# An encoder layer in split float32: weight slots of 1024 columns, 64-byte pads, and scale vectors and x loaded in quarters from another queue

## The chip, the core and the metric

The kernel runs on one core of a Trainium2 chip. The metric is the device time of one execution in microseconds (us), less is better. Three runs of the kernel before took 1114.95, 1115.65 and 1116.01 us, so the median is 1115.65 us. In the profile, PE is TensorE (matmuls), PEld its weight loads, DVE VectorE, ACT ScalarE, POOL GpSimd and SP the queue that issues most DMAs.

## The reference: what is computed

One layer on 256 rows of 2048 numbers, all float32:

```python
xn   = rmsnorm(x, pre_mix_gain)
proj = xn @ w_in                              # 2048 -> 3*1024 (hyena) + 832 (MLA)
y_hyena = x0 * long_conv(x1 * v, filters)     # by products with DFT tables
y_attn  = mla(c_q, c_kv, k_pe)                # 8 heads
mixed = concat(rmsnorm(y_hyena), rmsnorm(y_attn)) @ w_out        # 2048 x 2048
h  = x + rmsnorm(mixed, post_mix_gain)
gu = rmsnorm(h, pre_ffn_gain) @ w_up                             # 2048 x 11264
f  = (gelu(dwconv(gu[:, :5632])) * gu[:, 5632:]) @ w_down        # 5632 x 2048
y  = h + rmsnorm(f, post_ffn_gain)
```

## The kernel before, in words

Every operand of a large product is split into a high part (`...h`, or index 0) and a rest (`...l`, or index 1), and a product is three matmuls: high by high, high by rest, rest by high. In a matmul one operand is stationary (a 128x128 tile, loaded into the array by a PEld instruction ahead of each matmul) and the other is moving (it streams through, 256 or 512 columns here).

Weights come in tiles of 128 x 1024 float32 (512 KB). `stage` loads one with a DMA on SP into a slot `raw`, ACT copies it into a slot `wh` (L140), DVE subtracts to fill a slot `wl` (L143). There are four slots of each kind, used in turn; a slot is filled again when its last reader is done. The slots `wh` and `wl` are `W_SLOT` = 1040 columns wide, 4160 bytes in each partition, of which 1024 columns are used.

The stages, in order of time, with PE's work in them:

- MLA projection (to 52 us): `mm3` (L100 to L102), x stationary, weights moving.
- Hyena projection `hi` (52 to 262 us): `wm3` (L113 to L115), weights `why` stationary, x (`xT`) moving, 256 columns each; 48 weight tiles of 24 matmuls. Attention and the DFT products of the long convolution run between them.
- `w_out` (259 to 357 us), in two halves of 1024 output columns: `mm3`, the normalised mixer output (`mix`) stationary, weights moving, 512 columns; 12 matmuls for each of 16 tiles in a half.
- Residual and norm (352 to 381 us): `row_finish`, `post_mix`; they read the scale vectors `gbm` and `gbn` and the residual x (in tiles `h`).
- `w_up` (358 to 860 us): for n from 1 on, `wmm` (L108: 512 columns; L109: 256 columns), weights `wup` stationary, `hnT` moving; four weight tiles for each of 43 n, 64 matmuls.
- `w_down` (860 to 1105 us): `mm3` as in `w_out`, `fT` stationary, weights moving, 512 columns; 2 halves of 44 tiles, 12 matmuls each.

Each engine runs its instructions in the order in which the code emits them; the chains of attention and hyena are generators that are advanced between weight tiles (`turn`). POOL has, in this order around 250 to 300 us: sums of squares `sqh` (L547), the DMA of `gbm` (L873), `sqh`, the DMA of `gbn` (L875), `sqh`, two powers (L154) for the norm of the hyena output, and two DMAs of x into `h` (L877). A DMA whose target was used by earlier tiles waits for their readers, and what is behind it on its queue waits too.

Of the kernel before, what the change touches and what calls it, by code (L numbers as in the profile page):

```python
# [12 lines left out]
F32 = mybir.dt.float32  # L13
F32R = mybir.dt.float32r
# [4 lines left out]
P = 128  # L19
D = 2048  # L20
S = 256
# [7 lines left out]
NF = DFF // P  # L29
# [20 lines left out]
V_FCB = 274  # L50
V_ALL = 318
V_PAD = 320
W_SLOT = 1024 + 16


def _body(ctx, tc, a):
    nc = tc.nc
# [6 lines left out]

    const = ctx.enter_context(tc.tile_pool(name="const", bufs=1))
    edge = ctx.enter_context(tc.tile_pool(name="edge", bufs=1, side="right"))
    edge.tile([P, 24], F32, name="edge")
    wp = ctx.enter_context(tc.tile_pool(name="wp", bufs=4))
    psA = ctx.enter_context(tc.tile_pool(name="psA", bufs=2, space=bass.MemoryType.PSUM))
    psB = ctx.enter_context(tc.tile_pool(name="psB", bufs=3, space=bass.MemoryType.PSUM))  # L70
# [59 lines left out]

    def load(src, n, name):
        raw = wp.tile([P, 1024], F32, tag="raw", name=name)
        nc.sync.dma_start(raw[:, :n], src)
        return raw

    def split_w(raw, n, name, pool=None, cut=None):
        pool = pool or wp
        h = pool.tile([P, W_SLOT], F32R, tag="wh", name=name + "h")
        l = pool.tile([P, W_SLOT], F32R, tag="wl", name=name + "l")
        box["cast"] = nc.scalar.copy(h[:, :n], raw[:, :n])  # L140
        for e, o in ((nc.vector, slice(0, cut or n)), (nc.gpsimd, slice(cut or n, n))):
            if o.start < n:
                box["lo"] = e.tensor_tensor(l[:, o], raw[:, o], h[:, o].bitcast(F32), op=ALU.subtract)  # L143
        return h, l
# [21 lines left out]
    box = {}  # L166
# [13 lines left out]
    yp = l_stack.enter_context(tc.tile_pool(name="yp", bufs=1, side="left"))  # L180
    spec = l_stack.enter_context(tc.tile_pool(name="spec", bufs=1, side="left"))
    xTp = l_stack.enter_context(tc.tile_pool(name="xTp", bufs=1, side="left"))
    xT = [xTp.tile([P, 2, 2, P], F32R, name=f"xT{k}") for k in range(KD)]
    ya = [yp.tile([P, S], F32, name=f"ya{i}") for i in range(8)]
    yh = [yp.tile([P, S], F32, name=f"yh{i}") for i in range(8)]
# [15 lines left out]
    x = a["x"]  # L201
# [114 lines left out]
    for k in range(KD):  # L316
# [7 lines left out]
        wh, wl = wm[k]  # L324
# [423 lines left out]
    def channel_norm(sq, ys, gv, mix, nm, ps):  # L748

        rb = ps(f"rb{nm}")  # L750
        ps = ps(f"css{nm}")
        for b in range(2):
            nc.tensor.matmul(ps[:, b : b + 1], lhsT=sq[:, b * P : (b + 1) * P], rhs=ones[:, 0:1],
                             start=True, stop=True)
        r = [rms_scale(ps[:, b : b + 1], 1024, f"rn{nm}{b}", mixp) for b in range(2)]
        yield
        if nm == 'a':
            yield from pause(4)
        for b in range(2):
            bcast_rows(rb, r[b], b, mixp, "n" + nm)  # L760
        for i in range(8):
            with tc.issue_after(box["lo"].ins):
                nc.vector.scalar_tensor_tensor(ys[i], ys[i], vc(gv + i), rb[:, 0:S], op0=ALU.mult, op1=ALU.mult)
                split((mix[i][:, 0, :], mix[i][:, 1, :]), ys[i])
            if nm == "a" and i in (1, 3, 5):
                yield
# [3 lines left out]
    def attention_chain():  # L770
        nonlocal mixp, mix
        yield from latents()
        yield from attention()
        yield from pause(2)
        at_stack.close()
        mixp = mix_stack.enter_context(tc.tile_pool(name="mixp", bufs=1, side="right"))
        mix = [mixp.tile([P, 2, S], F32R, name=f"mix{k}") for k in range(KD)]
        yield from channel_norm(sqa, ya, V_AG, mix[0:8], "a", mi)

    mixp = mix = None  # L780
# [6 lines left out]
    for i, gi in order:  # L787
        for c in range(2):
            ps = (acc if cv else mj)(f"hi{i}{gi}{c}")[:, :S]
            for kh in range(2):  # L790
                wh, wl = stage(a["w_hy"][i, gi, c, kh], 1024, f"why{i}{gi}{c}{kh}")
                for kk in range(8):
                    k = kh * 8 + kk
# [8 lines left out]
    def row_units(wname, nk, half, lT, ps, hold, held):  # L802
        def get(k):
            return stage(a[wname][half, k], 1024, f"{wname}{half}{k}")

        nxt = get(0)
        for k in range(nk):
            w, nxt = nxt, get(k + 1) if k + 1 < nk else None
            for b in range(2):
                if b == 1 and k >= nk - hold:  # L810
                    held.append((k, w))
                    continue
                for c in range(2):
                    row_emit(ps[b][c], lT, k, b, w, c, nk)
            yield
# [38 lines left out]
    units = row_units("w_out", KD, 0, mix, psw, 0, None)  # L854
# [8 lines left out]
    h = [hp.tile([P, D], F32, name=f"h{b}") for b in range(2)]  # L863
    rb2 = hp.tile([P, S], F32, name="rb2")
    hn_stack = es()
    hnp = hn_stack.enter_context(tc.tile_pool(name="hnp", bufs=1, side="left"))
    hnTq = [hnp.tile([P, 4, 2, 2, P], F32R, name=f"hnT{c}") for c in range(4)]
    hnT = [hnTq[k // 4][:, k % 4] for k in range(KD)]
    pm_stack = es()
    pm = pm_stack.enter_context(tc.tile_pool(name="pm", bufs=1, side="left"))  # L870
    up0 = pm_stack.enter_context(tc.tile_pool(name="up0", bufs=4, side="left"))
    gbm = pm.tile([P, D], F32, name="gbm")
    nc.gpsimd.dma_start(gbm, a["post_mix_gain"].partition_broadcast(P))  # L873
    gbn = pm.tile([P, D], F32, name="gbn")
    nc.gpsimd.dma_start(gbn, a["pre_ffn_gain"].partition_broadcast(P))  # L875
    for b in range(2):
        nc.gpsimd.dma_start(h[b], x[b * P : (b + 1) * P, :])  # L877
    tmp = [pm.tile([P, D], F32, name=f"tmp{b}") for b in range(2)]
    ssq = [small(pm, 4, name=f"ssq{b}") for b in range(2)]
    ss2 = [small(pm, 4, name=f"ss2{b}") for b in range(2)]  # L880
    for _ in units:
        pass
    for b in range(2):
        for c in range(2):
            row_finish(psw, 0, b, c, gbm, tmp, ssq, pm)
# [26 lines left out]
    held = []  # L912
    psw = row_banks(1, "wo1")
    for k, _ in enumerate(row_units("w_out", KD, 1, mix, psw, HOLD, held)):
        if k == KD - HOLD - 2:
            first = [stage(a["w_up"][0, kq], 1024, f"wup0{kq}", up0) for kq in range(4)]
    row_finish(psw, 1, 0, 0, gbm, tmp, ssq, pm)
# [12 lines left out]
    fq = fpa_stack.enter_context(tc.tile_pool(name="fq", bufs=2, side="right"))  # L930
    fpa = fpa_stack.enter_context(tc.tile_pool(name="fpa", bufs=1, side="right"))
    NFA = 12
    def gated_tiles(pool, ks):
        for k in ks:
            if k % 4 == 0:
                pool.tile([P, 16], F32, name=f"fpad{k}")
            yield pool.tile([P, 2, S], F32R, name=f"fT{k}")

    fT = list(gated_tiles(fpa, range(NFA)))

    def up_tail(n, pg, pu):

# [49 lines left out]
    for n in range(1, NF):  # L992
        if n == 4:
            fpb = fpa_stack.enter_context(tc.tile_pool(name="fpb", bufs=1, side="right"))
            fT += gated_tiles(fpb, range(NFA, NF))
        new = (mi, mj) if n % 2 else (acc, acc)
        pg, pu = as4(new[0](f"pg{n}")), as4(new[1](f"pu{n}"))
        chs = []
        for kq in range(4):
            with es() as hold:  # L1000
                if n == 1:
                    for eng in range(2):
                        hold.enter_context(tc.issue_after(box[int(kq >= 2), 3, eng].ins))
                chs.append(stage(a["w_up"][n, kq], 1024, f"wup{n}{kq}"))
        for which, ps in ((0, pg), (1, pu)):
            for k in range(KD):
                wh, wl = chs[k // 4]
                o = (k % 4) * 256 + which * P
                wmm(ps, wh[:, o : o + P], wl[:, o : o + P], hnT[k], k == 0, k == KD - 1)
        up_tail(n, pg, pu)  # L1010
# [136 lines left out]
```

## Time and profile before

| | |
|---|---|
| median of three runs | 1115.65 us |
| the profiled execution | 1114.86 us, of which the span is 1113.1 us |
| PE busy | 1096.4 us (99%), 6334 matmuls |
| PEld busy | 959.4 us (86%) |
| DVE, ACT, POOL busy | 725.8 us (65%), 574.3 us (52%), 122.3 us (11%) |
| granted TensorE clock, mean | 0.997 |
| DMA | 207 MB, 186 GB/s over the span |

A share of the span is a mean over stages with different limits. A matmul's recorded time runs from its start to the end of its pipeline and overlaps the next one; what it costs in a row of matmuls is the distance from its start to the next start. The recorded times of two matmuls of one shape differ by as much as these distances do.

### The profile page before, as it was taken

To read this page: it belongs to the slowest core of one execution; us is meant where nothing else is said; L and a number is where in the kernel's file an instruction comes from. 1 tells how busy PE (TensorE), PEld (TensorE's weight loads), DVE (VectorE), ACT (ScalarE), POOL (GpSimd) and SP (SyncE) were. 2 spreads that over 40 slices of the span, in tenths; PEclk is the share of its full clock that TensorE was granted. 3 is DMA by queue.
4 is the path that set the end of the run, shared out by engine and by line. 5 is a ranking of instruction groups with operands and counts; after the bars stand their busy time and mean duration, and the time that the engine had idled before them with its cause. 6 is when DMAs were issued, how large, how long until landed. Compare 5 with 4: busy or idle time off the path is not lost.

```text
span 1113.1 us, 16496 instructions
## 1 busy us (share of the span) xinstructions
PE 1096.4 (99%) x6334; PEld 959.4 (86%) x6334; DVE 725.8 (65%) x1051; ACT 574.3 (52%) x884; POOL 122.3 (11%) x154
## 2 busy tenths in 40 slices
PE   9999999999999999999999999999999999999997
PEld 7899999998787888888888888888888888888885
DVE  7898878889567766666666666565756444454444
ACT  7756656655454646454545455554545333343332
POOL 4300100011002311111111111111111000000000
PEclk9999999999999999999999999999999999999999
DMA  9664445444775354645464645555555766666652
GB/s 312 224 212 148 161 133 171 143 136 131 276 253 189 114 190 162 216 157 219 156 214 164 204 176 197 182 188 191 179 199 172 258 188 191 189 192 188 189 191 95
DMA packets 59207, 207.23 MB, mean 186 GB/s; under 512 B 6903, under 2 KB 7801, under 8 KB 58489
## 3 DMA queue, kind: packets, MB, share of 16 engines
q1 hardware_dynamic: 57832, 200.39, 54.1%
q0 software_dynamic: 720, 5.24, 1.3%
q8 instruction: 49, 0.80, 0.3%
q10 hardware_dynamic: 576, 0.56, 0.1%
q14 instruction: 30, 0.24, 0.1%
HBM read 204.07 MB, written 2.10 MB: 185 GB/s over the span
## 4 chain that ended last, share of the span: by engine, by line
PE 86%; issue 6%; DVE 5%; DMA 1%; POOL 1%; ACT 1%; DVEq 0%; POOLq 0%; SPq 0%; ACTq 0%
PE pg L108 14%; PE pu L108 14%; PE pg L109 7%; PE pu L109 7%; PE wd L102 7%; PE wd L100 7%; PE wd L101 7%; PE hi L113 4%; PE hi L115 4%; PE hi L114 4%; DMA w_out<-in_w_out 1%; POOL tmp L893 1%; PE y L499 1%; PE pq L101 1%; PE pq L100 1%
## 5 line engine op out<-in xcount | busy, mean ns | idle before, releaser
L91 ACT CAST fT<-u 128x256 fp32r<-128x256 f32 x44 | 17.8, 406 | 111.1 <-DVE u L952 111.0
L551 DVE SCALAR_TENSOR_TENSOR t<-g,vec,t 128x255 f32<-128x255 f32 x44 | 21.3, 483 | 63.8 <-ACT t L550 63.8
L948 POOL TENSOR_TENSOR u<-u,rb 128x256 f32<-128x256 f32 x44 | 32.4, 736 | 276.4 <-DVE u L125 276.4
L550 ACT ACTIVATE t<-g,vec 128x256 f32<-128x256 f32 x44 | 26.5, 603 | 54.9 <-POOL g L946 54.9
L125 DVE TENSOR_TENSOR g<-pg,jg 128x256 f32<-128x256 f32 x44 | 18.7, 424 | 52.5 <-ACT jg L124 52.5
L946 POOL TENSOR_TENSOR g<-g,rb 128x256 f32<-128x256 f32 x44 | 32.4, 736 | 137.6 <-DVE g L125 136.2
L124 ACT COPY jg<-pg 128x256 f32<-128x256 f32 x44 | 16.3, 371 | 54.7 <-PE pg L109 54.7
L952 DVE TENSOR_TENSOR u<-u,t 128x256 f32<-128x256 f32 x44 | 18.7, 424 | 36.4 <-POOL u L948 35.4
L834 POOL TENSOR_TENSOR rw0r<-rw0v,neghalf 128x1 f32<-128x1 f32 x2 | 1.1, 558 | 292.1 <-DVE rw0v L831 292.1
L92 DVE TENSOR_TENSOR fT<-u,fT 128x256 fp32r<-128x256 f32 x44 | 18.7, 425 | 19.8 <-ACT fT L91 19.8
L553 DVE SCALAR_TENSOR_TENSOR t<-g,vec,t 128x255 f32<-128x255 f32 x44 | 21.3, 484 | 1.5
L547 POOL TENSOR_TENSOR sqa<-sqa,sqa 128x256 f32<-128x256 f32 x7 | 6.8, 965 | 128.9 <-ACT sqa L546 128.6
L951 ACT ACTIVATE t<-t 128x256 f32<-128x256 f32 x44 | 18.2, 414 | 2.7 <-DVE t L553 2.7
L125 DVE TENSOR_TENSOR u<-pu,ju 128x256 f32<-128x256 f32 x44 | 18.3, 417 | 0.0
L550 ACT ACTIVATE cv<-z,vec 128x256 f32<-128x256 f32 x24 | 14.4, 601 | 7.5 <-DVE z L616 7.5
L232 POOL TENSOR_TENSOR sqx<-sqx,sqx 128x256 f32<-128x256 f32 x15 | 15.7, 1047 | 17.8 <-ACT sqx L231 17.6
L124 ACT COPY ju<-pu 128x256 f32<-128x256 f32 x44 | 16.0, 364 | 0.0
L96 DVE SCALAR_TENSOR_TENSOR xT<-xraw,vec,xT 128x256 fp32r<-128x256 f32 x16 | 11.8, 740 | 2.7 <-ACT xT L95 2.7
L893 POOL TENSOR_TENSOR tmp<-h,gbn 128x512 f32<-128x512 f32 x8 | 13.3, 1682 | 2.4 <-DVE h L890 2.4
L616 DVE TENSOR_TENSOR z<-hi,rbx 128x256 f32<-128x256 f32 x24 | 10.0, 418 | 5.2 <-PE hi L115 4.9
L547 POOL TENSOR_TENSOR sqh<-sqh,sqh 128x256 f32<-128x256 f32 x7 | 7.8, 1114 | 47.6 <-ACT sqh L546 47.5
L553 DVE SCALAR_TENSOR_TENSOR cv<-z,vec,cv 128x255 f32<-128x255 f32 x24 | 12.4, 518 | 0.2
(3679 smaller groups left out, 4378.0 us busy)
## 6 DMA issues: line engine op xcount, KB each, us to landing
wup<-in_w_up SPq DMA_DIRECT2D x176, 512.0 KB, 4.8
w_down<-in_w_down SPq DMA_DIRECT2D x88, 512.0 KB, 3.5
why<-in_w_hy SPq DMA_DIRECT2D x48, 512.0 KB, 3.9
w_out<-in_w_out SPq DMA_DIRECT2D x32, 512.0 KB, 4.3
wm<-in_w_mla SPq DMA_DIRECT2D x16, 416.0 KB, 4.9
win<-in_window SPq DMA_DIRECT2D x8, 256.0 KB, 3.1
wuq<-in_w_uqn SPq DMA_DIRECT2D x4, 512.0 KB, 3.5
wkv<-in_w_ukv SPq DMA_DIRECT2D x4, 512.0 KB, 4.1
```

What stands on the lines that cost most here:

```text
L100: ins = nc.tensor.matmul(ps, lhsT=lh, rhs=rh, start=first, stop=False)
L101: nc.tensor.matmul(ps, lhsT=lh, rhs=rl, start=False, stop=False)
L102: nc.tensor.matmul(ps, lhsT=ll, rhs=rh, start=False, stop=last)
L108: nc.tensor.matmul(ps, lhsT=wh, rhs=xt, start=first, stop=False)
L109: nc.tensor.matmul(ps[:, :, 0, :], lhsT=wl, rhs=xt[:, :, 0, :], start=False, stop=last)
L113: nc.tensor.matmul(ps, lhsT=wh, rhs=xt[:, :, 0, :], start=first, stop=False)
L114: nc.tensor.matmul(ps, lhsT=wh, rhs=xt[:, :, 1, :], start=False, stop=False)
L115: box["mm"] = nc.tensor.matmul(ps, lhsT=wl, rhs=xt[:, :, 0, :], start=False, stop=last)
L125: nc.vector.tensor_add(d, ps4[:, :, 0, :], lo)
L550: nc.scalar.activation(dst, src, AF.Identity, bias=vc(bv), scale=vc(wv + 1))
L553: nc.vector.scalar_tensor_tensor(dst[:, : S - 1], src[:, 1:], vc(wv + 2), dst[:, : S - 1], op0=ALU.mult, op1=ALU.add)
L946: nc.gpsimd.tensor_tensor(g, g, rb2, op=ALU.mult)
```

## The change

`W_SLOT` goes: the slots `wh` and `wl` become 1024 columns, 4096 bytes. Pads of 16 columns (64 bytes) are allocated ahead of `xT` and `hnT`, behind `mix` and behind the first twelve `fT`; the pad at the right edge grows from 24 to 40 columns, and a pad ahead of every four `fT` goes. So the addresses of nearly all tiles move by multiples of 64 bytes. No arithmetic, no matmul and no copy is added or removed, and PE, DVE and ACT have the same instructions in the same order.

Counted from the addresses that the two built programs give, here is the byte address of the moving operand minus that of the stationary one, modulo 256, in matmuls of each stage:

| stage | before | after |
|---|---|---|
| MLA projection | 0, 64, 128, 192, a quarter each | 192 |
| `hi` (1152 matmuls) | 0 (312), 64 (288), 128 (264), 192 (288) | 64 |
| DFT products `K`, `AB`, `yc` (144) | 0 | 64 |
| `w_out` (384) | 0, 64, 128, 192, a quarter each | 0 |
| `w_up`, n from 1 on (2752) | 0, 64, 128, 192, a quarter each | 64 |
| `w_down` (1056) | 0, 64, 128, 192, a quarter each | 0 |

Before, the distance is the same within a weight tile and changes with the slot, by 64 from one tile to the next. In `w_up` the tiles of one n (`wup80`, `wup81`, `wup82`, `wup83` for n = 8) have the distances 128, 192, 0 and 64. In `w_out`, the tiles 0 and 1 of the second half (`w_out10` and `w_out11`; the first digit is the half) have 0 and 192. In `w_down`, the tiles 1 and 2 of the first half (`w_down01`, `w_down02`) have 64 and 0. In `hi`, `why2001` has 0, and `why2101` and `why1200` both have 64.

The second part: `gbm`, `gbn` (1 MB each) and x (2 MB into `h`) are loaded by SP in quarters of the vectors and halves of x's row blocks, one behind each of twelve `w_out` loads, and no longer by POOL in four whole DMAs.

```diff
-W_SLOT = 1024 + 16
...
-    edge.tile([P, 24], F32, name="edge")
+    edge.tile([P, 40], F32, name="edge")
...
-        nc.sync.dma_start(raw[:, :n], src)
+        box["load"] = nc.sync.dma_start(raw[:, :n], src)
...
-        h = pool.tile([P, W_SLOT], F32R, tag="wh", name=name + "h")
-        l = pool.tile([P, W_SLOT], F32R, tag="wl", name=name + "l")
+        h = pool.tile([P, 1024], F32R, tag="wh", name=name + "h")
+        l = pool.tile([P, 1024], F32R, tag="wl", name=name + "l")
...
+    xTp.tile([P, 16], F32, name="xpad")
     xT = [xTp.tile([P, 2, 2, P], F32R, name=f"xT{k}") for k in range(KD)]
...
         mix = [mixp.tile([P, 2, S], F32R, name=f"mix{k}") for k in range(KD)]
+        mixp.tile([P, 16], F32, name="mpad")
...
+    hnp.tile([P, 16], F32, name="hpad")
     hnTq = [hnp.tile([P, 4, 2, 2, P], F32R, name=f"hnT{c}") for c in range(4)]
...
-    nc.gpsimd.dma_start(gbm, a["post_mix_gain"].partition_broadcast(P))
     gbn = pm.tile([P, D], F32, name="gbn")
-    nc.gpsimd.dma_start(gbn, a["pre_ffn_gain"].partition_broadcast(P))
-    for b in range(2):
-        nc.gpsimd.dma_start(h[b], x[b * P : (b + 1) * P, :])
+
+    def piece(dst, src, c, n):
+
+        o = slice(c * n, (c + 1) * n)
+        with tc.issue_after(box["load"].ins):
+            nc.sync.dma_start(dst[:, o], src[:, o])
...
-    for _ in units:
-        pass
+    for k, _ in enumerate(units):
+        if k < 4:
+            piece(gbm, a["post_mix_gain"].partition_broadcast(P), k, 512)
...
     for k, _ in enumerate(row_units("w_out", KD, 1, mix, psw, HOLD, held)):
+        if k < 4:
+            piece(h[k // 2], x[k // 2 * P : (k // 2 + 1) * P, :], k % 2, 1024)
+        elif k < 8:
+            piece(gbn, a["pre_ffn_gain"].partition_broadcast(P), k - 4, 512)
...
-    def gated_tiles(pool, ks):
-        for k in ks:
-            if k % 4 == 0:
-                pool.tile([P, 16], F32, name=f"fpad{k}")
-            yield pool.tile([P, 2, S], F32R, name=f"fT{k}")
-
-    fT = list(gated_tiles(fpa, range(NFA)))
+    fT = [fpa.tile([P, 2, S], F32R, name=f"fT{k}") for k in range(NFA)]
+    fpa.tile([P, 16], F32, name="fpad")
```

POOL's order before, from the second half of the sums of squares to the scaling of the residual:

```order
L547 TENSOR_TENSOR sqh_124<-sqh_124,sqh5_3394 128x256
L873 DMA gbm_3854<-in_post_mix_gain 128x2048
L547 TENSOR_TENSOR sqh_124<-sqh_124,sqh6_3691 128x256
L875 DMA gbn_3856<-in_pre_ffn_gain 128x2048
L547 TENSOR_TENSOR sqh_124<-sqh_124,sqh7_3696 128x256
L154 TENSOR_TENSOR rnh0r_3759<-rnh0v_3757,neghalf_77 128x1
L154 TENSOR_TENSOR rnh1r_3763<-rnh1v_3761,neghalf_77 128x1
L877 DMA h0_3838<-in_x 128x2048
L877 DMA h1_3839<-in_x 128x2048
L834 TENSOR_TENSOR rw0r_4320<-rw0v_4318,neghalf_77 128x1
```

The same place of POOL in the changed kernel:

```order
L547 TENSOR_TENSOR sqh_125<-sqh_125,sqh5_3396 128x256
L547 TENSOR_TENSOR sqh_125<-sqh_125,sqh6_3693 128x256
L547 TENSOR_TENSOR sqh_125<-sqh_125,sqh7_3698 128x256
L153 TENSOR_TENSOR rnh0r_3761<-rnh0v_3759,neghalf_77 128x1
L153 TENSOR_TENSOR rnh1r_3765<-rnh1v_3763,neghalf_77 128x1
L835 TENSOR_TENSOR rw0r_4331<-rw0v_4329,neghalf_77 128x1
```

The four DMAs are gone from POOL, and the sums and powers stand behind one another.

SP's order before, at the loads of the first tiles of the second half of `w_out` (`w_out11` is tile 1 of half 1):

```order
L133 DMA w_out11_4028<-in_w_out 128x1024
L133 DMA w_out12_4046<-in_w_out 128x1024
L133 DMA w_out13_4064<-in_w_out 128x1024
L133 DMA w_out14_4082<-in_w_out 128x1024
L133 DMA w_out15_4100<-in_w_out 128x1024
L133 DMA w_out16_4118<-in_w_out 128x1024
```

The same place of SP in the changed kernel:

```order
L132 DMA w_out11_4031<-in_w_out 128x1024
L881 DMA h0_3840<-in_x 128x1024
L132 DMA w_out12_4050<-in_w_out 128x1024
L881 DMA h0_3840<-in_x 128x1024
L132 DMA w_out13_4069<-in_w_out 128x1024
L881 DMA h1_3841<-in_x 128x1024
L132 DMA w_out14_4088<-in_w_out 128x1024
L881 DMA h1_3841<-in_x 128x1024
L132 DMA w_out15_4107<-in_w_out 128x1024
L881 DMA gbn_3858<-in_pre_ffn_gain 128x512
L132 DMA w_out16_4126<-in_w_out 128x1024
```

Each of the loads of tiles 2 to 9 of this half now stands behind a piece of x or of `gbn`; in the same way the loads of tiles 10 to 13 of the first half stand behind a quarter of `gbm`.

## Rows read from the trace of the kernel before

**Rows 1.** The page's chain that ended last: shares of the span by engine.

```profile
PE 86%; issue 6%; DVE 5%; DMA 1%; POOL 1%; ACT 1%; DVEq 0%; POOLq 0%; SPq 0%; ACTq 0%
```

**Rows 2.** Windows: stretch, its us, busy us of each engine, clock, DMA, GB/s.

```profile
52.90:264.00 211.10, 211.08 (x1737) 208.55 (x1736) 181.24 (x324) 128.03 (x225) 13.94 (x14) 1.00 0.48 151
381.55:860.42 478.87, 478.87 (x2723) 417.46 (x2721) 304.99 (x429) 250.94 (x388) 64.00 (x87) 1.00 0.53 185
860.54:1104.58 244.04, 244.04 (x1057) 198.07 (x1056) 113.65 (x104) 94.22 (x101) 1.91 (x3) 1.00 0.60 188
```

**Rows 3.** Timeline of PE in `w_out`: start us, us recorded, engine, line, tiles.

```profile
311.57 0.39 PE L100 MATMUL wo<-w_out10h,mix 128*128 128x512 f32 x1
...
312.73 0.39 PE L102 MATMUL wo<-w_out10h,mix 128*128 128x512 f32 x1
...
314.32 0.39 PE L100 MATMUL wo<-w_out11h,mix 128*128 128x512 f32 x1
...
317.12 0.39 PE L100 MATMUL wo<-w_out12h,mix 128*128 128x512 f32 x1
```

**Rows 4.** Timeline of PE in `w_down`, the first matmul of three weight tiles.

```profile
863.31 0.39 PE L100 MATMUL wd<-w_down01h,fT 128*128 128x512 f32 x1
...
866.05 0.40 PE L100 MATMUL wd<-w_down02h,fT 128*128 128x512 f32 x1
...
868.83 0.39 PE L100 MATMUL wd<-w_down03h,fT 128*128 128x512 f32 x1
```

**Rows 5.** Groups by form in `w_up`, n = 8: busy us, mean ns of one.

```profile
L108 PE MATMUL pg<-hnT,wup82h 128*128 128x512 f32 x4 | 1.5, 400 | 0.0
...
L108 PE MATMUL pg<-hnT,wup81h 128*128 128x512 f32 x4 | 1.5, 395 | 0.0
...
L108 PE MATMUL pg<-hnT,wup83h 128*128 128x512 f32 x4 | 1.4, 395 | 0.0
L108 PE MATMUL pg<-hnT,wup80h 128*128 128x512 f32 x4 | 1.4, 393 | 0.0
...
L109 PE MATMUL pg<-hnT,wup80l 128*128 128x256 f32 x4 | 1.1, 282 | 0.0
L109 PE MATMUL pg<-hnT,wup82l 128*128 128x256 f32 x4 | 1.1, 282 | 0.0
...
L109 PE MATMUL pg<-hnT,wup81l 128*128 128x256 f32 x4 | 1.1, 282 | 0.0
...
L109 PE MATMUL pg<-hnT,wup83l 128*128 128x256 f32 x4 | 1.1, 280 | 0.0
```

**Rows 6.** One tile, `wup82h`: ns min/median/max, first and last start.

```profile
L108 PE MATMUL pg<-hnT,wup82h x4: 395/400/404, 457.7 to 458.8; 128*128 128x512 f32 x4
```

**Rows 7.** Tiles of `hi`, the same view: `why2001h`, `why2101h`, `why1200h`, `why1200l`.

```profile
L113 PE MATMUL hi<-xT,why2001h x8: 283/283/283, 146.7 to 149.2; 128*128 128x256 f32 x8
...
L113 PE MATMUL hi<-xT,why2101h x8: 276/276/276, 165.5 to 167.9; 128*128 128x256 f32 x8
...
L113 PE MATMUL hi<-xT,why1200h x8: 279/279/279, 181.6 to 184.1; 128*128 128x256 f32 x8
...
L115 PE MATMUL hi<-xT,why1200l x8: 277/280/280, 181.9 to 184.3; 128*128 128x256 f32 x8
```

**Rows 8.** The chain of waits, 272 to 297 us: start us, us, what.

```profile
274.20 11.57 DMA w_out<-in_w_out
```

**Rows 9.** Timeline of POOL, DVE and PE there, idle before and releaser in brackets.

```profile
272.61 0.75 POOL L873 DMA_DIRECT2D gbm<-in_post_mix_gain  x1 [20.75 <-DMA w_out<-in_w_out]
...
283.22 1.22 DVE L143 TENSOR_TENSOR w_out08l<-w_out,w_out08h 128x1024 fp32r<-128x1024 f32 x1 [4.84 <-ACT w_out08h L140]
...
285.62 0.92 PE L161 MATMUL rbh<-dgnh,ones 128*128 128x128 f32 x4 [0.81 <-DVE dgnh L160]
```

**Rows 10.** Windows at the loads of x; columns as in Rows 2.

```profile
295.00:309.00 14.00, 14.00 (x62) 11.40 (x61) 5.98 (x6) 3.48 (x4) 1.12 (x2) 1.00 0.88 328
```

**Rows 11.** Timeline of ACT in the second half of `w_out`.

```profile
322.86 1.05 ACT L140 CAST w_out17h<-w_out 128x1024 fp32r<-128x1024 f32 x1 [1.70 <-PE wo L102]
```

More of the change, by code (lines that the diff above doesn't have):

```diff
@@ L994, in _body @@
             fpb = fpa_stack.enter_context(tc.tile_pool(name="fpb", bufs=1, side="right"))
-            fT += gated_tiles(fpb, range(NFA, NF))
+            fT += [fpb.tile([P, 2, S], F32R, name=f"fT{k}") for k in range(NFA, NF)]
         new = (mi, mj) if n % 2 else (acc, acc)
```

## The prediction

> **What bounds the kernel.** I read the chain of waits first: 86% of the span in it is PE [rows 1]. The windows of the three long stages say why: in the hyena projection, in w_up and in w_down PE is busy for the whole stretch at the full granted clock, and DVE, ACT and DMA have room [rows 2]. So in these 930 us no wait is left to remove, and what counts is the distance from one matmul's start to the next, times their number. Outside them I looked for waits of PE that the moved DMAs could cause or cure.
>
> The starts show that equal matmuls do not cost the same. In w_out, two weight tiles of 12 equal matmuls take 314.32-311.57 = 2.75 and 2.80 us [rows 3], in w_down two take 2.74 and 2.78 [rows 4]. By the address distances listed with the change, w_out's two have 0 and 192, and w_down's 64 and 0. In w_down the stationary tiles lie at ever new addresses too, so it may be the difference of both addresses that orders these times: PEld is busy for 208.55 of 211.10 us in the hyena stretch [rows 2], so the next stationary tile is read while the moving one streams, and the two can meet. In w_up the four tiles of one n differ in the same way: L108 and L109 together have 393+282 = 675 at distance 128, 400+282 = 682 at 0 and 395+280 = 675 at 64; the fourth, at 192, has 395+282 = 677 [rows 5]. In the hyena projection a matmul is recorded with 283 ns at distance 0 and 276 at 64 [rows 7].
>
> Within a tile the time is not constant either, and this decides most of the sum. The distance-0 tile of w_out needs (312.73-311.57)/5 = 232 ns for each of its first five matmuls, and (314.32-312.73)/7 = 227 for the last seven [rows 3]: after a change of distance the pattern needs some matmuls to settle, and then it stays. The hyena tiles show that one distance can have two settled patterns: both at 64, why2101 has 276 and why1200 279 to 280 [rows 7]. So the mean over four slots is a mean over unsettled patterns, and with one distance each stage should run in one settled pattern.
>
> **The change part by part.** PE, DVE and ACT keep their instructions and order, so the first part only replaces these distances.
>
> 1. w_down: 1056 matmuls, 244.04 us over 1055 starts, 231.3 ns each [rows 2]. All get distance 0, settled 227 [rows 3]: 4.3 x 1055 = 4.5 us less. Bounds: if it never settles, the w_down tile at 0 has 2.78/12 = 231.7, no gain; as w_out's tile at 192, 2.80/12 = 233.3, a loss of 2.1 us.
> 2. w_out: 384 matmuls, also at 0. No window holds this stage alone, so I use the same 4.3 ns: 4.3 x 384 = 1.7 us, of which I take 1.2, since in its first half the hyena chain's matmuls come between and the pattern has to settle again. Bounds 0.8 us more (at 233.3) and 1.7 less.
> 3. w_up: 478.87 us for about 2720 matmuls, so 352.1 ns for an L108 with its L109 [rows 2]. The mean of the four sums is (675+677+682+675)/4 = 677.25, the sum at 64 is 675: 2.25 x 1376 pairs = 3.1 us less. A settled pattern at 64 is not to be seen here, as four pairs are too few. From below, I take the settled 227 for L108 and for L109 the mean less the best hyena difference, 352.1-(232-227)-(283-276) = 340: 16.5 us less. From above, the sum at 0: 4.75 x 1376 = 6.5 us more. I take the tile at 64, the only row with that distance and this pair.
> 4. Hyena: 1152 matmuls, all at 64. In before, 312 are at distance 0 with 283 ns, and 288 at 64 with 276 or, over the three lines of its tile, (279+279+280)/3 = 279.3 (L114 as L113) [rows 7]; the 552 at 128 and 192 I put between 276 and 283, at 280, which makes a mean of 280.4. Which pattern the stage will run in, no row tells. I take the slow one: 1.1 ns, 1.3 us less. Bounds: all fast 5.1 us less, all at 283 3.0 us more.
> 5. The DFT products: 144 matmuls from 0 to 64, 283-279.3 = 3.7 ns each: 0.5 us less; bounds 0 and 1.0. The MLA projection gets 192 throughout; at 2 ns over the mean its 192 matmuls would lose 0.4 us if PE alone bounded it; I take 0.
>
> The DMAs. In before, POOL's DMA of gbm starts at 272.61 us [rows 9] and that of gbn stands one sum behind it: 2 MB that run beside the w_out loads, one of which then takes 11.57 us [rows 8]. So DVE idles 4.84 us until it can make w_out08l, the scale of the hyena norm is queued behind that on DVE, and PE waits 0.81 us for dgnh [rows 9]. In the changed kernel nothing but the w_out loads runs at that moment, as the first quarter of gbm is issued behind tile 9. I take 1.0 us less: the wait and its ramp. Bounds 0 (another load is late in its place) and 1.6 us (twice the wait).
>
> What they cost: SP issues twelve DMAs more, and behind each waits a w_out load. In the second half, x and gbn add 3 MB within eight tiles. With 512 KB more for a tile, 1 MB is due in the 2.75 us of PE's tile; the rate while x was loaded before, 328 GB/s over 14 us [rows 10], needs 3.2 us, so four tiles fall behind by 1.8 us together, and the four with a quarter of gbn (2.4 us each) catch up. The cover is that loads run ahead: ACT's cast of w_out17 waits for PE to free a slot, by 1.70 us, and not for its load [rows 11], and from cast to PE's use are three more tiles. I take 0; with no cover it would be 3.1 MB / 328 = 9.6 us. gbm, x and gbn are needed only behind the halves' last matmuls.
>
> Equal work at other addresses differs by 2% in the tiles above [rows 3, 5]. Here the Trainium skill speaks against the change: TensorE: Matmul & The Clock Gate, section Step-by-step: what each phase is for, says that the stationary and the moving operand come through two independent read ports of SBUF. By it addresses would cost nothing, and only the 1.0 us of the DMAs would be left. The trace does not agree; what it leaves open is only whether the distance or something else of the slot is the cause, and that is rival A.
>
> The sum: 4.5+1.2+3.1+1.3+0.5+1.0 = 11.6 us. The profiled execution took 1114.86 (its span of 1113.1 and 1.8 around it), so 1103.3; it lies 0.8 us under the median of the runs, so against the median I say 1104.
>
> **Rivals.**
>
> A. The distance does nothing. The slots differ for another reason, such as their place in the four-tile cycle, and all tiles keep their times. Against it: w_out and w_down order their tiles by the distance at different slots. Only the DMAs' 1.0 us is left: 1114.6.
>
> B. w_up settles in a better pattern than its tile at 64 shows. Its tile gives 352.1-2.25 = 350 ns a pair, its bound is 340. Halfway, at 345, it saves 6.7 us more than step 3: 1097.
>
> C. w_up settles in a worse one, as the tile at 0 (682): 6.5 us more in place of 3.1 less, so 1113.6. For it: hyena's two patterns at 64.
>
> D. Slower: w_up locks in its slowest single pair. In the tile at 0, L108 goes from 395 up to 404 [rows 6]; with 404+282 = 686 every time, the pair is 8.75 ns over the mean, 12.0 us more in place of 3.1 less: 1119. It decides from 358.3 ns a pair on, where w_up loses the 8.5 us that the other steps win. Against it: even at 0 the mean is only 682.
>
> E. SP is the new wait: the pieces hold up w_out's loads, PE runs dry in the second half. Half of the 9.6 us exposed: 1108.8; all of it 1113.6. Against it the cover above.
>
> **How the numbers follow.** Forecast 0.52 (own range 1100 to 1107: steps 3 and 4 vary by 3 us), B 0.20, C 0.10, A 0.06, D 0.06, E 0.06. The range takes in the forecast, B (to 8 us under the forecast) and E's half, and leaves out the far ends of steps 3 and 4 below, and A, C and D above: 1096 to 1111. Two runs of this kernel differ by up to 0.1%, so 0.2% (2.2 us) is what can be told. Faster, below 1113.4: forecast, B, half of C and most of E, 0.83. Same, to 1117.9: half of C, A and some of E, 0.12. Slower: D less its mild cases, 0.05.
>
> **What would show it.** w_down's window: 1055 starts in 239.5 us if step 1 is right, 244 if wrong. In w_up, L108 and L109 of all four tiles of an n should have the same means, and their sum tells step 3 from B, C and D: 675 against 670, 682 and 686. If the four tiles still differ as before, A is right. In the hyena tiles 276 or 279 to 280, and no 283. In POOL no DMA between the sums of squares; no long w_out load in the chain and no wait of PE for dgnh, which is the DMA term. E would show as ACT's casts of w_out12 to w_out19 waiting for DMA and PE behind them. Wrong altogether I would be if a stage settled slower than its four-slot mean, which no row of a whole tile at its new distance shows.

## The result and the profile after

The changed kernel took 1100.01 us (median of 4 runs, 1098.23 to 1105.85) against 1115.3 us: ratio 0.9872, 95% interval 0.9833 to 0.991. The forecast was 1104 in 1096 to 1111. Its runs spread over 7.6 us; those of the kernel before lie within 1.2 us. The profiled execution took 1101.09 us with a span of 1099.3, so 13.8 us less than the profiled one of before. In its chain of waits PE has still more of the span than in [rows 1]:

```profile
PE 91%; DVE 4%; issue 2%; ACT 1%; DMA 1%; POOL 1%; DVEq 0%; POOLq 0%; SPq 0%; ACTq 0%
```

The windows between the same matmuls as in [rows 2] (columns as there): hyena with its products, w_up, w_down; the last row is the 14 us in which x is loaded, as [rows 10].

```profile
53.37:262.75 209.38, 209.08 (x1735) 206.50 (x1736) 181.34 (x325) 127.71 (x224) 13.94 (x14) 1.00 0.49 152
377.29:851.91 474.62, 474.62 (x2722) 415.64 (x2721) 305.23 (x429) 251.10 (x388) 64.20 (x87) 1.00 0.54 187
852.02:1091.20 239.18, 239.18 (x1058) 198.03 (x1056) 113.56 (x104) 94.50 (x102) 2.03 (x3) 1.00 0.63 191
294.00:308.00 14.00, 14.00 (x63) 11.61 (x62) 6.92 (x7) 6.64 (x10) 0.00 (x0) 1.00 0.96 354
```

Against [rows 2], w_up has 4.3 us less and w_down 4.9. The hyena window of [rows 2] ends 0.1 us ahead of the matmul that ends this one, which starts at 264.10 before; up to that start hyena has 1.8 us less. Between hyena and w_up, the same two matmuls stand 117.45 us apart before (264.10 to 381.55) and 114.55 after:

```profile
262.75:377.30 114.55, 109.83 (x545) 91.68 (x544) 79.83 (x110) 58.71 (x94) 20.48 (x16) 0.99 0.64 216
```

That is 2.9 us. The hyena stretch begins 0.5 us later (53.37 for 52.90), and from the last matmul's start to the span's end it is 8.1 us for 8.5. So -0.5 + 1.8 + 2.9 + 4.3 + 4.9 + 0.4 = 13.8 us, which is all of it. In w_down the tiles start 2.72 us apart, each of them, where they had 2.74 and 2.78 [rows 4]:

```profile
854.78 0.39 PE L99 MATMUL wd<-w_down01h,fT 128*128 128x512 f32 x1
...
857.50 0.39 PE L99 MATMUL wd<-w_down02h,fT 128*128 128x512 f32 x1
...
860.22 0.39 PE L99 MATMUL wd<-w_down03h,fT 128*128 128x512 f32 x1
```

2.72 / 12 = 226.7 ns from the first tile to the last. In w_up the four tiles of n = 8 now agree (grouped by form, as [rows 5]; L107 and L108 are before's L108 and L109):

```profile
L107 PE MATMUL pg<-hnT,wup81h 128*128 128x512 f32 x4 | 1.4, 394 | 0.0
L107 PE MATMUL pg<-hnT,wup80h 128*128 128x512 f32 x4 | 1.4, 393 | 0.0
L107 PE MATMUL pg<-hnT,wup82h 128*128 128x512 f32 x4 | 1.4, 393 | 0.0
L107 PE MATMUL pg<-hnT,wup83h 128*128 128x512 f32 x4 | 1.4, 393 | 0.0
L108 PE MATMUL pg<-hnT,wup82l 128*128 128x256 f32 x4 | 1.1, 281 | 0.0
L108 PE MATMUL pg<-hnT,wup81l 128*128 128x256 f32 x4 | 1.1, 280 | 0.0
L108 PE MATMUL pg<-hnT,wup83l 128*128 128x256 f32 x4 | 1.1, 280 | 0.0
L108 PE MATMUL pg<-hnT,wup80l 128*128 128x256 f32 x4 | 1.1, 280 | 0.0
```

The hyena tiles of [rows 7]:

```profile
L113 PE MATMUL hi<-xT,why2001h x8: 279/279/279, 146.6 to 149.0; 128*128 128x256 f32 x8
...
L113 PE MATMUL hi<-xT,why2101h x8: 280/280/280, 165.0 to 167.4; 128*128 128x256 f32 x8
...
L113 PE MATMUL hi<-xT,why1200h x8: 276/276/276, 181.1 to 183.5; 128*128 128x256 f32 x8
...
L114 PE MATMUL hi<-xT,why1200l x8: 276/276/276, 181.2 to 183.6; 128*128 128x256 f32 x8
```

No tile has 283 any more, but 276 and 280 stand side by side, at one distance and in one execution. By starts, 31 of the 49 stretches of one tile have 117.7 ns a matmul and 18 have 113.3. Which tile has which is not as before: why2101 and why1200 have changed places [rows 7].

POOL, DVE and PE at the sums of squares, as [rows 9]:

```profile
270.87 4.23 POOL L547 TENSOR_TENSOR sqh<-sqh,sqh 128x256 f32<-128x256 f32 x2 [20.36 <-ACT sqh L546]
...
278.45 1.23 DVE L142 TENSOR_TENSOR w_out08l<-w_out,w_out08h 128x1024 fp32r<-128x1024 f32 x1 [1.49 <-ACT w_out08h L139]
...
283.08 0.61 PE L160 MATMUL rbh<-dgnh,ones 128*128 128x128 f32 x4
```

POOL has no DMA between the sums, DVE idles 1.49 us for 4.84, and PE no longer waits for dgnh. ACT's cast of w_out17h waits for PE, as in [rows 11]:

```profile
319.10 1.05 ACT L139 CAST w_out17h<-w_out 128x1024 fp32r<-128x1024 f32 x1 [1.67 <-PE wo L101]
```

### The profile page after: what moved, and what is told of

It reads as the page before. It is cut to its first block, busy times and chain, and to the rows that moved or that the text cites. A ratio compares the mean times of both kernels' runs of the same rounds, so it can differ in the third digit from the quotient of the medians.

```text
span 1099.3 us, 16503 instructions
## 1 busy us (share of the span) xinstructions
PE 1083.8 (99%) x6334; PEld 956.1 (87%) x6334; DVE 725.8 (66%) x1051; ACT 574.3 (52%) x884; POOL 123.3 (11%) x150
## 4 chain that ended last, share of the span: by engine, by line
PE 91%; DVE 4%; issue 2%; ACT 1%; DMA 1%; POOL 1%; DVEq 0%; POOLq 0%; SPq 0%; ACTq 0%
PE pg L107 14%; PE pu L107 14%; PE pg L108 7%; PE pu L108 7%; PE wd L100 7%; PE wd L99 7%; PE wd L101 7%; PE hi L113 4%; PE hi L112 4%; PE hi L114 4%; PE wo L100 2%; PE wo L101 2%; PE wo L99 2%; PE y L499 1%; DMA why<-in_w_hy 1%
```

## The experiments

The times of stages below are sums over the stage's matmuls, each from its start to PE's next start (w_down's goes from its first start to its last). For w_up they hold 2752 matmuls and are 6.5 us more than the windows. Those of hi hold 14 pauses of 0.08 us and one of 0.2 us, in every kernel alike. A "pair" is a matmul of w_up with 512 columns (L107) and the one with 256 (L108) behind it. "Distance" is the moving tile's address less the stationary tile's, modulo 256.

**e1_addr**, the addresses alone:

```diff
+    nc.gpsimd.dma_start(gbm, a["post_mix_gain"].partition_broadcast(P))
+    nc.gpsimd.dma_start(gbn, a["pre_ffn_gain"].partition_broadcast(P))
+    for b in range(2):
+        nc.gpsimd.dma_start(h[b], x[b * P : (b + 1) * P, :])
-        if k < 4:
-            piece(gbm, a["post_mix_gain"].partition_broadcast(P), k, 512)
...
-            piece(h[k // 2], x[k // 2 * P : (k // 2 + 1) * P, :], k % 2, 1024)
-        elif k < 8:
-            piece(gbn, a["pre_ffn_gain"].partition_broadcast(P), k - 4, 512)
```

> The addresses alone: every distance of moving to stationary tile as in the changed kernel, but gbm, gbn and x again loaded by POOL in four whole DMAs. Theory (the distance sets the pattern of a stage): w_down 239 us from first to last start, a pair of L107 and L108 in w_up 349 ns, hi and the other stages as in the changed kernel; about 1 us more than the changed kernel, 1101 us, all of it in w_out (a late w_out08 load, a wait of PE for dgnh). Rival (the moved DMAs carry the gain, the slots only differ among themselves): w_down 244 us, 352 ns a pair, about 1114 us.

1105.53 us, ratio 0.9916 (0.99 to 0.9933). Its windows of w_up and w_down:

```profile
378.30:858.82 480.52, 480.52 (x2723) 418.64 (x2721) 305.09 (x429) 251.02 (x388) 64.10 (x87) 1.00 0.54 184
858.93:1098.11 239.18, 239.18 (x1057) 198.02 (x1056) 113.51 (x104) 94.82 (x101) 1.91 (x3) 1.00 0.61 191
```

w_down has the changed kernel's time to the hundredth, so the addresses make it. w_up has not: 480.52 for 474.62, at the same addresses. DVE waits 4.29 us for w_out08's cast again, and PE waits for dgnh.

**e2_dma**, the moved DMAs alone; against the kernel before:

```diff
-    nc.gpsimd.dma_start(gbm, a["post_mix_gain"].partition_broadcast(P))
...
+            piece(gbm, a["post_mix_gain"].partition_broadcast(P), k, 512)
...
+            piece(h[k // 2], x[k // 2 * P : (k // 2 + 1) * P, :], k % 2, 1024)
```

> The moved DMAs alone: gbm, gbn and x by SP in pieces, slots and pads as before, so every stage has its four distances in turn. Theory: 1 us less than before, 1114.3 us, all in w_out; w_down stays at 244 us and the pair at 352 ns. Rival (the DMAs carry the gain): 1105 us or less. Second rival (the pieces delay w_out's loads, and only the faster matmuls of the changed kernel paid for it): 1116 to 1120 us.

1111.34 us, ratio 0.9971 (0.996 to 0.9983): 3.7 us, not 1. w_up and w_down have before's windows, 478.86 and 244.06, so the rival falls, but the term was too small. In the trace PE's start of the first rbh matmul comes 1.0 us earlier against its neighbour, the four rbh take 0.61 us for 0.92, and two pairs of late starts behind them go (0.2 and 0.3 us): 1.7 to 1.9 us. The end is 0.4 us shorter, 8.1 for 8.5, and so in every kernel whose pieces go by SP; e1_addr has 8.5. Why, no row shows. The two profiled executions lie 4.1 us apart; 1.5 us of that are the clock, below, and 0.4 us come ahead of hi.

**e3_again**, the changed kernel unaltered (no diff):

> The changed kernel once more, unaltered: its four runs spread from 1098.2 to 1105.9 us, those of the kernel before from 1114.8 to 1116.0. Theory: the same addresses settle in different patterns from one execution to the next, so the spread stays at several us, and where this profile's total differs from the first one's, one stage differs as a whole (hi by up to 4.4 ns a matmul, 5 us, or w_up by some ns a pair). Rival (something outside the program, as a slow DMA): the spread is gone, or the difference lies in waits at single places.

1103.97 us (1098.99 to 1108.14). This profile's windows of w_up and w_down:

```profile
376.59:857.12 480.53, 480.53 (x2723) 418.79 (x2722) 305.09 (x429) 251.15 (x388) 64.28 (x87) 1.00 0.53 184
857.23:1096.39 239.16, 239.16 (x1057) 198.08 (x1056) 113.50 (x104) 94.83 (x101) 2.04 (x3) 1.00 0.61 191
```

The theory holds. The same kernel has 474.62 us in one execution and 480.53 in another, and PE sits idle in neither. Its tiles of n = 8 agree with one another again, a few ns higher than in the first profile:

```profile
L107 PE MATMUL pg<-hnT,wup81h 128*128 128x512 f32 x4 | 1.5, 396 | 0.0
...
L108 PE MATMUL pg<-hnT,wup80l 128*128 128x256 f32 x4 | 1.1, 283 | 0.0
```

By starts, three pairs repeat: 349, 347 and 351 ns in the one (mean 348.9), 348, 357 and 355 in the other (353.3). From n = 3 to n = 43 neither changes. Where the pattern is decided can be seen at one weight load. In each of the 14 profiles PEld's first load of wup23l (n = 2) waits for DVE and starts 0.05 us behind DVE's end, while in the rest of w_up every first load of such a tile comes 0.5 us or more behind its own. In the first profile, and then in this one:

```profile
385.62 1.76 DVE L142 TENSOR_TENSOR wup23l<-wup,wup23h 128x1024 fp32r<-128x1024 f32 x1
...
387.43 0.19 PEld L108 LDWEIGHTS pg<-hnT,wup23l 128*128 128x128 f32 x1
```

```profile
384.91 1.75 DVE L142 TENSOR_TENSOR wup23l<-wup,wup23h 128x1024 fp32r<-128x1024 f32 x1
...
386.72 0.19 PEld L108 LDWEIGHTS pg<-hnT,wup23l 128*128 128x128 f32 x1
```

Four profiles have distance 64 in w_up: these two, e1_addr and e7_shift. Just ahead of this load all four run at 353.3 ns a pair. Where PEld sat idle before it for 72 ns (first profile) and 50 ns (e7_shift), they run at 348.9 from there on; where it did for 34 and 35 ns (this one, e1_addr), they stay at 353.3. That the length of this wait chooses the pattern fits all four, and was not tested.

The second difference between the two profiles is in w_out, where PE waits for w_out01l in both, 2.1 us from start to start. The windows behind that wait, first of the first profile, then of this one:

```profile
264.00:268.00 4.00, 2.58 (x7) 2.04 (x8) 4.00 (x8) 1.00 (x3) 0.00 (x0) 0.72 0.39 104
268.00:272.00 4.00, 4.00 (x17) 3.23 (x16) 4.00 (x7) 1.54 (x3) 1.13 (x1) 0.85 0.79 219
```

```profile
264.00:268.00 4.00, 2.16 (x12) 1.62 (x11) 4.00 (x8) 2.15 (x5) 0.00 (x0) 1.00 0.15 18
268.00:272.00 4.00, 4.00 (x19) 3.27 (x19) 4.00 (x9) 1.47 (x2) 0.00 (x0) 1.00 0.73 242
```

In the first the granted clock falls below 1.00 and some seven or eight matmuls start 427 ns apart in place of 227 to 236, so at the lower level of 1.2 GHz: 8 x 0.2 = 1.6 us. In the second it stays at 2.4 GHz. Of the 14 profiles, 7 show the fall there and 7 do not (before does, e2_dma does not), after 2.08 to 2.12 us from start to start each time.

**e4_swap**, other pads:

```diff
-    xTp.tile([P, 16], F32, name="xpad")
...
-        mixp.tile([P, 16], F32, name="mpad")
+        mixp.tile([P, 32], F32, name="mpad")
...
-    hnp.tile([P, 16], F32, name="hpad")
...
-    fpa.tile([P, 16], F32, name="fpad")
+    fpa.tile([P, 32], F32, name="fpad")
```

> Only pads changed: distance 0 in place of 64 in hi, the DFT products and w_up, and 64 in place of 0 in w_out and w_down. Theory: w_down settles as the kernel before's tiles at 64 did, 2.74 to 2.76 us for 12, 229 ns each, 241.6 us in place of 239.2; w_out 0.8 us more; hi as the earlier tiles at 0, 283 in place of 279.5 ns recorded, 3.5 x 1152 = 4 us more at most; w_up by its earlier tile at 0 (682 against 675 for the pair's two recorded times) up to 7 ns a pair and 9.6 us more, or, if the sum of the two settled matmuls counts (227 + 120 at 0, 229 + 118 at 64), no change. In all 1107 us without and 1117 with the 9.6. Rival (only the slots' equal cycle matters, not the distance): 1100 us, every stage as in the changed kernel.

1113.83 us. w_down 241.49 us and hi 4.3 us more, as the theory had it; w_up 486.95 (353.3 ns a pair), which the changed kernel has too in its slower pattern. The slots are those of the changed kernel, and the time is nearly that of the kernel before.

**e5_d128** and **e6_d192**, the same four pads (`xpad`, `hpad`, `mpad`, `fpad`) of 32, 32, 48, 48 and of 48, 48, 0, 0 columns; of the second:

```diff
-    xTp.tile([P, 16], F32, name="xpad")
+    xTp.tile([P, 48], F32, name="xpad")
...
-        mixp.tile([P, 16], F32, name="mpad")
```

> Only pads changed: distance 128 in every stage with weight tiles. Theory (each stage settles by its distance, and its whole tiles of before at that distance bound it): w_down's earlier tiles at 128 took 2.77 to 2.80 us for 12, so 231 to 233.5 ns each, 244 to 246 us in place of 239.2; w_up's pair somewhere between its two patterns at 64 (349.0, 353.3) and not beyond 355, the stage 481 to 489 us; hi about 118.7 ns, 1.5 us more. Together 1106 to 1117 us. Rival (one distance in a stage is enough, whichever it is): w_down 239 us, hi 135 us, total as the changed kernel's 1098 to 1108 us.

> Only pads changed: distance 192 in hi, w_up, w_out and w_down (64 in the MLA projection). Theory: w_down as its earlier tiles at 192, 2.795 to 2.801 us for 12, 233.2 ns each, 246 us in place of 239.2; w_out 6 ns x 384 = 2.3 us more; hi as at 64 or faster (its earlier tiles at 192 and 64 have the same two recorded times, 276 and 279 to 280); w_up's pair 349 to 354. Together 1106 to 1118 us, the slowest of the four for w_down. Rival (one distance in a stage is enough): w_down 239 us, total 1098 to 1108 us.

1112.98 and 1115.48 us. The windows of hyena, w_up and w_down at 192:

```profile
53.79:262.32 208.53, 208.44 (x1735) 205.87 (x1736) 181.26 (x325) 127.83 (x224) 13.92 (x14) 1.00 0.48 152
378.76:859.29 480.53, 480.53 (x2723) 417.39 (x2721) 305.32 (x429) 251.28 (x388) 64.15 (x87) 1.00 0.53 184
859.40:1105.57 246.17, 246.17 (x1057) 197.29 (x1056) 113.78 (x104) 94.18 (x101) 2.02 (x3) 1.00 0.59 186
```

So one distance in a stage is not the gain. At 192, w_up and w_down are slower than with before's four distances in turn, though hyena is the fastest of all. At 128 w_down has 245.17 and w_up 484.0, inside what was expected; hi, 3.0 us more for 1.5, is not (its 118.8 ns a matmul are near the 118.7 expected, but the mean that they were set against holds the pauses).

**e7_shift**, every tile 64 bytes further at the same distances:

```diff
-    edge.tile([P, 40], F32, name="edge")
+    edge.tile([P, 24], F32, name="edge")
+    const.tile([P, 16], F32, name="cpad")
```

> Every tile of the changed kernel moved by 64 bytes (16 columns more among the constants, 16 fewer in the pad at the right edge), so all distances are the changed kernel's and all addresses modulo 256 are not. Theory (the difference counts): w_down 239.2 us, hi 134.9 to 135.2, w_up one of the two patterns, 481.1 or 487.0 us; 1098 to 1108 us. Rival (an address by itself counts, of the stationary or of the moving tile): stages settle as in the kernels whose tiles lie 64 bytes further, w_down 241.5 to 246 us, and w_up at neither 349.0 nor 353.3 ns.

1098.28 us; w_down 239.16, w_up 481.09, hi 134.99. The rival falls: it is the difference of the two addresses.

**e8_fine**, the four pads of 8, 8, 24 and 24 columns:

```diff
-    xTp.tile([P, 16], F32, name="xpad")
+    xTp.tile([P, 8], F32, name="xpad")
```

> Only pads changed: distance 32 in hi, w_up, w_out and w_down (half a step of 64). Theory 1 (steps of 64 count, what lies between falls to the step below): as distance 0, w_down 239.2 us, hi 139.5 us, w_up 487 us, 1107 us. Theory 2 (steps finer than 64 count): patterns that none of the four distances showed, w_down between 239 and 246 us. Rival (to the step above): as 64, w_down 241.5 us, hi 135 us, w_up 481 or 487.

1105.73 us. w_down 246.16 (as at 192), w_up 478.14 (346.7 ns a pair, in which none of the four distances settled), hi 136.15. Steps finer than 64 count: w_down has 233.3 ns at 32, and 226.7 and 228.9 on either side.

**e9_h0_l64** and **e10_h64_l0**, a pad between the two kinds of slots, of 48 and of 16 columns, with `xpad` of 32 columns in the first, and neither `xpad` nor `hpad` in the second:

```diff
+        if pool is wp and "lpad" not in box:
+            box["lpad"] = pool.tile([P, 48], F32, tag="lpad", name="lpad", bufs=1)
         l = pool.tile([P, 1024], F32R, tag="wl", name=name + "l")
```

> A pad of 192 bytes between the wh and the wl slots: in w_up the matmul with wh (512 columns) has distance 0 and the one with wl (256 columns) 64. Theory 1 (what counts is a matmul's moving tile against its own stationary tile): L107 settles at 227 ns as w_down does at 0, L108 at 113 to 118 as hi does at 64: 340 to 345 ns a pair, 468 to 475 us for w_up in place of 481 or 487. Theory 2 (the moving tile against the next stationary tile, loaded meanwhile): L107 then meets wl at 64, 229 ns or more, L108 meets wh at 0, 120 ns: 349 to 353 ns, 481 to 487 us. In w_down the middle one of three matmuls moves to 192 and costs up to 6 ns, 2.1 us in all. Rival (the pattern of w_up depends on nothing that a distance sets): 349 or 353.3 ns, as the two profiles of the changed kernel.

> A pad of 64 bytes between the wh and the wl slots, and none ahead of hnT: in w_up the matmul with wh (512 columns) has distance 64 and the one with wl (256 columns) 0. Theory 1 (own stationary tile counts): 229 + 120 = 349 ns a pair or more, 481 to 487 us for w_up. Theory 2 (the next stationary tile counts): L107 meets wl at 0, 227 ns, L108 meets wh at 64, 113 to 118 ns: 340 to 345 ns, 468 to 475 us. In w_down the middle one of three matmuls moves to 64 and costs about 2 ns, 0.7 us in all. Rival (no distance sets it): 349 or 353.3 ns.

1099.57 and 1110.84 us. The window of w_up in e9_h0_l64:

```profile
376.38:848.04 471.66, 471.66 (x2723) 411.68 (x2721) 305.04 (x429) 250.91 (x388) 64.28 (x87) 1.00 0.55 188
```

A pair settles at 346.7 ns, between the two theories: L108 has the 113.3 of theory 1, but L107 has 233.3 where it should have 227. e10_h64_l0 runs at 340.0 ns a pair, the figure of theory 2, in the 19 pairs ahead of the load of wup23l, before which PEld sits idle longer than in any other run:

```profile
390.11 0.19 PEld L108 LDWEIGHTS pg<-hnT,wup23l 128*128 128x128 f32 x1 [0.39 <-DVE wup23l L144]
```

Behind it, it runs at 350.0 to the end; e9_h0_l64 goes from 351.1 to 346.7 there. So one pair of distances has two patterns in one execution, and neither theory tells which one stays: the time of a settled pair is not the sum of what its matmuls take alone. w_down, where one in three is displaced, has 241.48 and 244.75 us (0.7 more was expected in the second, 5.6 came).

**e11_best** and **e12_best**: e9_h0_l64, and `l` of w_down's tiles from the fifth on in a second pool of four slots at distance 0; `xpad` of 32 and of 16 columns:

```diff
+    wq = ctx.enter_context(tc.tile_pool(name="wq", bufs=4, side="left"))
+    box["fin"] = wq
...
+            if "fin" in box and half + k // 4:
+                box["wq"] = box["fin"]
...
-        l = pool.tile([P, 1024], F32R, tag="wl", name=name + "l")
+        l = box.get("wq", pool).tile([P, 1024], F32R, tag="wl", name=name + "l")
```

> The kernel with wh at 0 and wl at 64 in w_up (346.7 ns a pair there), and in w_down from its fifth tile on wl in four slots of its own at distance 0, in the space that hnT leaves. Theory (the pattern follows from the distances each time): w_up 478.1 us, w_down 239.2 to 239.5 in place of 241.5; 1097.3 us in executions whose clock stays up in w_out, 1.6 more in the others; the six runs within 1096 to 1100, so a smaller spread than the changed kernel's 1098 to 1108. Rival 1 (346.7 was only one of two patterns of these distances): some runs 5 us or more slower. Rival 2 (the new slots wait for hnT's last reader and PE runs dry at w_down's start): a wait of 1 to 3 us of PE there, 1099 to 1101 us.

> As e11_best, but the pad ahead of xT is 64 bytes and not 128, so in hi the two matmuls with wh have distance 0 and the one with wl 64 (in e11_best 64 and 128). Theory (in a sequence the distances act together, as in w_up, where wl at 64 beside wh at 0 gave 113 ns): hi's third matmul 113 to 114 ns and the first two 120 or less, so 117.5 to 118 at most and 116 at best: 133.6 to 135.9 us; total within 1.5 us of e11_best. Rival (each matmul by its own distance): (120 + 120 + 117.7) / 3 = 119.2 ns, 137.3 us, 2.4 us slower than e11_best.

e11_best: 1101.35 us (1095.74 to 1105.53, 6 runs), ratio 0.988 (0.986 to 0.99); profiled at 1095.74, the lowest time of all. e12_best: 1100.91 (1098.56 to 1105.27, 5 runs), 0.9874 (0.9853 to 0.9894). The windows of w_up and w_down in e11_best:

```profile
374.72:846.38 471.66, 471.66 (x2722) 411.85 (x2721) 304.97 (x429) 250.89 (x388) 64.04 (x87) 1.00 0.54 188
846.49:1085.78 239.29, 239.29 (x1057) 198.09 (x1056) 113.53 (x104) 94.91 (x102) 2.04 (x3) 1.00 0.60 191
```

In the profile w_up and w_down are as the theory has it, and PE does not wait at w_down's start. But the runs spread over 9.8 us, no less than the changed kernel's, as rival 1 says, and the median is not told apart from the changed kernel's. These distances do have a second pattern: in both profiles w_up runs at 351.1 ns a pair ahead of the load of wup23l, 4.4 ns more than behind it. Whether that takes the time in the longer runs isn't seen, as only one run of each is profiled. In e12_best hi has 137.09 us, which looks like the rival's 137.3. But 1.3 us of it are the pauses, which neither figure held. Without them a matmul takes 117.9 ns, the most that the theory allowed, and less than the rival's 119.2: the two with wh take 118.8 and 119.0, and the one with wl 115.7. So here too the distances act together.

The pattern that each stage settled in, from the profiles (ns a matmul; for w_up ns a pair, behind the load of wup23l; hi without the pauses, w_out without its waits):

| distance | hi | w_up pair | w_out | w_down |
|---|---|---|---|---|
| four in turn (before) | 117.4 | 352.1 | 231.2 | 231.3 |
| 0 | 119.9 | 353.3 | 227.1 | 226.7 |
| 32 | 117.0 | 346.7 | 233.3 | 233.3 |
| 64 | 116.1 | 348.9 or 353.3 | 229.1 | 228.9 |
| 128 | 118.8 | 351.1 | 232.3 | 232.4 |
| 192 | 115.4 | 353.3 | 233.3 | 233.3 |

Distance 0 is the best for w_down and the worst for hi. The column of w_up does not rank the distances: each but 64 has one profile, and ahead of the load of wup23l distance 0 ran at 346.7 ns a pair, no slower than 32.

## Why the prediction was right, step by step

1. w_down: 4.5 us expected, 244.05 to 239.16 = 4.9 found. The settled 227 ns that the last seven matmuls of w_out's tile showed [rows 3] is what the whole stage runs at. The step held, and e4_swap, e5_d128, e6_d192 and e7_shift show that the distance makes it. The 0.4 us over come from taking 227 for 226.7.
2. w_out: 1.2 expected; (231.2 - 227.1) x 384 = 1.6 us found. The full 4.3 ns would have been right: the hyena chain's matmuls between do not unsettle it.
3. w_up: 3.1 expected, 4.3 found in the first profile, and 1.6 us more than before (485.41 to 487.00) in that of e3_again. This is where the prediction was right by its mean only, and it was luck that the first profile fell on the quicker pattern. Its sentence that with one distance each stage should run in one settled pattern holds within an execution from n = 3 on, but the distance doesn't say which: 348.9 or 353.3. Rival C, settling in a worse pattern, happens in some executions, at a quarter of its price. The tile at 64 [rows 5] gave 350, which lies between and is neither.
4. hyena: 1.3 expected, 1.5 found. The step took the pattern of 279 to 280 for the whole stage, and the stage mixes it with 276, tile by tile. So "one settled pattern" fails here too, by little. The mean of 280.4 in the step comes out at 280.2 with half of the tiles at 64 in either pattern, which makes 1.1 us of the 1.3.
5. DFT products: 0.5 expected, 119.5 to 116.0 ns x 144 = 0.5 found. MLA: 0 expected; its matmuls take 38.3 us before, 37.7 in the first profile and 38.9 in that of e3_again, and most of the difference is PE's wait for a weight tile, wm9l (0.8, 0.2 and 0.7 us).

The DMAs: 1.0 expected. In the changed kernel 2.9 - 1.6 (step 2) = 1.3 between hyena and w_up, with the clock's fall in both profiles, and 0.4 at the end. Alone, e2_dma has 1.7 to 1.9 and 0.4. The mechanism was right, late load, DVE, dgnh, PE, and the size was off: the matmuls just behind the wait were slow too, and the step counted the wait and a small ramp. Rival E was not seen in w_out12 to w_out19 (the cast of w_out17 waits for PE); the cover held, with the loads at 354 GB/s where 328 had been measured.

Rival A is refuted by e4_swap, e5_d128 and e6_d192, which have the changed kernel's slots and took 1113.0 to 1115.5 us. Its rule, the two independent read ports in the Trainium skill (TensorE: Matmul & The Clock Gate, Step-by-step: what each phase is for), is not what this case shows: 226.7 and 233.3 ns for the same 1056 matmuls at distances 0 and 192. Rivals B and D did not occur in the four profiles at distance 64; 346.7 ns, near B's 345, came only at other distances.

The chance for "slower" was small and the range held, but two events move the result from one execution to the next, w_up's pattern (5.9 us) and the clock in w_out (1.5). The changed kernel's ten runs fall in two groups, six from 1098.2 to 1101.7 and four from 1105.9 to 1108.1, and the two profiled ones stand one in each, by their w_up pattern. That the eight others divide by the same cause is likely, and not shown. So it is in good part chance that the median of the first four runs lies 4 us under the forecast: three of them are in the quicker group, and the six of e3_again have 1103.97. What decides the pattern is open in part: the traces show where, at the one weight load that waits for DVE, and that the length of its wait chooses is not tested.

## What to carry to other kernels

Where PE is busy throughout and its clock is full, time equal matmuls by their starts: if equal work differs by a few per cent between tiles, sort them by the difference of the moving and the stationary address before anything else. Measure each stage at several distances, since the best differs by stage (0 for 512 columns alone; 192, in one profile, for 256 alone; none shown for the alternating pair). Profile one kernel more than once before a single profile is believed: here the same program had stages of 474.6 and 480.5 us. Look at the weight loads too, and not at PE's idle time alone: the load behind which the pattern changed is a wait that PE's row hardly shows.

## What the runs showed of the hardware

- The start-to-start time of a matmul depends on the moving address less the stationary one: 226.7 to 233.3 ns at 512 columns (w_down), 115.4 to 119.9 at 256 (hi, the mean of a stage). A move of both by 64 bytes left w_down's 239.16 us as they were (e7_shift). 32 bytes differ from 0 and from 64.
- One distance can have two stable patterns: 348.9 and 353.3 ns a pair at 64 in w_up, and, with 64 for wh and 0 for wl, 340.0 and then 350.0 in one execution (e10_h64_l0). The change comes at a weight load that waits for DVE, and w_up then stays in one pattern for 464 us. In hi, where other matmuls come between, it changes from tile to tile (113.3 and 117.7 ns).
- After PE's wait for w_out01l, at the start of w_out, the granted clock fell to the lower level in 7 of 14 profiles and stayed up in 7, in the same place and after the same time between starts to 0.04 us.
